# Output projection fed from a table, token sums in two pieces, and empty pulls in the final norm

## The chip, the cores and the metric

The kernel runs on one core of a Trainium2 chip. The metric is the device time of one execution in microseconds (us). The profile is of one such execution; its span runs from the program's first instruction to its last. TensorE (PE) does the matrix products, VectorE (DVE) and ScalarE (ACT) the elementwise work, GpSimd (POOL) some of it, and SyncE's queue (SP) issues all DMA transfers.

## The reference

One layer over 128 context tokens and 2048 latent tokens, 2176 in all, with a model width of 1024. Context and latent tokens get their own modulation vectors (`v` 0 or 1 in the kernel).

```python
h = rmsnorm(x, norm1) * (1 + scale1) + shift1
z = h @ w_in                       # short-convolution inputs, q, k, v, o, gates
y_sc = sc_b * conv3(sc_c * sc_x)   # along a row of 64 tokens
h_m = mlstm_bidir(q, k, v, gates)  # 4 heads, 16 chunks of 128 tokens, both directions
h_m = normed(h_m) * sigmoid(o)
x = x + gate1 * (concat([y_sc, h_m]) @ w_out)
h2 = rmsnorm(x, norm2) * (1 + scale2) + shift2
up = conv3(h2 @ w_up)              # down the columns of the grid
x = x + gate2 * ((silu(gg) * a) @ w_down)
y = rmsnorm(x, final_norm)
```

The final states of the context scan are returned too.

## The kernel before

Activations lie with features on the 128 partitions and tokens along the free dimension. Every float32 product is made of three: each operand is split into a rounded part (`H`, `wh`, by a copy on ACT) and a rest (`L`, `wl`, by a subtraction on VectorE or GpSimd), and high by high, high by low and low by high are summed in PSUM. `gemm` (L221 to L223) does this for 8 feature tiles and a block of up to 384 tokens, 24 products in all. There are six token blocks; the last has 256 tokens. Weights come through `load_w`: a DMA into `wst`, the copy `wh` on ACT (L127) and two half subtractions `wl` on GpSimd (L130).

The order of the front half. After the modulation and the first norm, blocks 3 to 5 and then 0 to 2 get their values, gates, keys, queries, output gates and short convolution. The last such stretch weaves two sequences. `weave` walks over units, calls the named stages of several units in the order of its list, and pulls items from a generator `fill` at a given rate. First the units are `Sums` (backward states) with the fill `heads` for queries and output gates; then they are `Mix` (one chunk and head pair each) at 1.6 items a unit, with the fill `shortconv` (36 items: four feature tiles by three blocks by three products) followed by `out_proj` (48 steps).

`out_proj` runs over three groups of two token blocks; a step is one `gemm` of one output tile for one block, and its eviction (L604) adds the residual row on VectorE. Its input, the mixed features in DRAM (`yD`), is loaded in two halves of four tiles, and split into `yH` and `yL` by `split_y`: four copies (L517) and four subtractions (L518) in a row. For blocks 0 and 1 `shortconv` calls this through `load_y`, for the others `out_proj` pulls `next_y`, four tiles at a time. `close` stores a finished row and squares it (L566), `add` sums the squares (L572), and `stats` makes the second norm's factors from them (L493 to L495).

From the first unit of `Mix` to the end of `out_proj`, `in_order` ties each engine, and SP's queue, to the order in which the code emits the instructions. Outside this stretch a planner orders each engine's instructions by priority and a cost model, with the emission order as the priority.

The up projection works with sums and differences of token and weight quarters, seven products in place of eight, in two halves of the tokens. `sums` forms the seven token forms for half of such a half (`qs`), in four rounds `kk`: load two stretches of `xD` into a tile `F`, norm and modulate them (L272, L274), form the differences (L276 to L279), split the ones named in `direct` into their slots (L283, L284) and store the rest to `tD` (L287). `split` loads a form from `tD` into `F` (L302) and splits it into its slot (L312, L313). The slots are used in the order 6, 0, 1, 5, 2, 4, 3. `F` has two buffers.

The down projection is built in the same way, in two groups `g` of seven products `i`, each over eight pairs `k` of output tile and token part. `close` adds the result to the residual and sums squares. `finish` makes the final norm of half a part: `inv_rms` (products L144, VectorE L147, a power on GpSimd L148), `spread` (products L155), and eight multiplications (L1331) with a store each. These generators are chained in `after`, and pulled four items at a time behind the products of each `k` from 2 on:

```python
if k >= 2:
    for _ in islice(after, 4):
        pass
```

## Time and profile before

| what | value |
|---|---|
| time, median of 3 runs | 2541.38 us (2538.63 to 2546.69) |
| profiled execution | 2547.02 us, its span 2545.2 us |
| mean granted TensorE clock | 0.987 |
| TensorE products busy | 2464.8 us, 97% of the span |
| VectorE, ACT, GpSimd busy | 1664.6, 1122.8, 573.7 us |

The profile names an engine's instruction by its line in the code and by the tiles it writes and reads. A wait is the idle time of an engine in front of an instruction and is put down to what released it. The granted clock is the share of full speed at which TensorE was allowed to run.

### The profile page before, as it was taken

How to read it: one execution, taken by the hardware profiler on the slowest of the kernel's cores; microseconds unless marked ns; L12 is line 12 of the kernel's file. 1: busy time of each engine (PE TensorE's matmuls, PEld its weight loads, DVE VectorE, ACT ScalarE, POOL GpSimd, SP SyncE). 2: the span in 40 equal slices, each digit the busy share in tenths (PEclk: the TensorE clock that was granted, in tenths of full speed). 3: DMA queues.
4: the chain of work that ended last, by engine and by line, in shares of the span. 5: the costliest groups of instructions: out<-in, count | busy, mean ns of one | idle time of the engine just before them, and what ended most of it. 6: DMA issues, size and time to landing. Idle time of an engine off the chain costs nothing.

```text
span 2545.2 us, 42525 instructions
## 1 busy us (share of the span) xinstructions
PE 2464.8 (97%) x16127; PEld 2360.4 (93%) x16127; DVE 1664.6 (65%) x2670; ACT 1122.8 (44%) x2059; POOL 573.7 (23%) x501
## 2 busy tenths in 40 slices
PE   7999999998999999889999999899999999999998
PEld 7999999998999989889999999788888899999998
DVE  3993552331556676688677666877767786787586
ACT  4421162333444554455444444555545554444342
POOL 2442242110343443322122111221221100000000
PEclk9999999999999999999999999999999999999999
DMA  8873873455666876755224122522222276867674
GB/s 282 279 241 116 305 242 96 126 177 166 209 208 204 285 243 221 250 199 174 83 99 165 73 74 83 183 98 84 92 98 84 80 248 207 251 195 225 188 222 133
DMA packets 281424, 444.60 MB, mean 175 GB/s; under 512 B 23283, under 2 KB 206723, under 8 KB 279555
## 3 DMA queue, kind: packets, MB, share of 16 engines
q1 hardware_dynamic: 281218, 441.88, 52.9%
q8 instruction: 127, 2.08, 0.3%
q14 instruction: 79, 0.64, 0.1%
HBM read 335.31 MB, written 106.48 MB: 174 GB/s over the span
## 4 chain that ended last, share of the span: by engine, by line
PE 68%; DVE 5%; DMA 4%; issue 2%; ACT 1%; POOL 0%; SPq 0%; DVEq 0%; ACTq 0%; POOLq 0%
PE pa L1206 7%; PE pa L1208 6%; PE pa L1207 6%; PE d L1361 5%; PE d L1362 5%; PE d L1360 5%; PE acc L221 4%; PE acc L223 4%; PE acc L222 4%; PE pb L1206 3%; PE pb L1207 3%; PE pb L1208 3%; PE pc L1206 2%; PE pc L1207 2%; PE pc L1208 2%
## 5 line engine op out<-in xcount | busy, mean ns | idle before, releaser
L221 PE MATMUL acc<-hH,wh 128*128 128x384 f32 (+1 forms) x1536 | 514.6, 335 | 23.3 <-DVE row L604 14.6
L223 PE MATMUL acc<-hH,wl 128*128 128x384 f32 (+1 forms) x1536 | 507.8, 331 | 0.4 <-POOL wl L130 0.4
L222 PE MATMUL acc<-hL,wh 128*128 128x384 f32 (+1 forms) x1536 | 506.7, 330 | 0.0
L1206 PE MATMUL pa<-tH,wh 128*128 128x288 f32 (+1 forms) x1056 | 348.7, 330 | 12.1 <-issue 7.3
L1360 PE MATMUL d<-bh,wh 128*128 128x272 f32 x1232 | 356.7, 290 | 0.7 <-ACT raw L1218 0.7
L1362 PE MATMUL d<-bh,wl 128*128 128x272 f32 x1232 | 357.1, 290 | 0.0
L1361 PE MATMUL d<-bl,wh 128*128 128x272 f32 x1232 | 356.3, 289 | 0.0
L1208 PE MATMUL pa<-tH,wl 128*128 128x288 f32 (+1 forms) x1056 | 347.9, 329 | 1.0 <-DVE wl L331 1.0
L1207 PE MATMUL pa<-tL,wh 128*128 128x288 f32 (+1 forms) x1056 | 347.6, 329 | 0.0
L331 POOL TENSOR_TENSOR wl<-st,wh 128x512 fp32r<-128x512 f32 x132 | 185.3, 1403 | 704.3 <-ACT wh L330 677.8
L130 POOL TENSOR_TENSOR wl<-wst,wh 128x512 fp32r<-128x512 f32 (+1 forms) x160 | 236.5, 1501 | 419.2 <-ACT wh L127 373.1
L221 PEld LDWEIGHTS acc<-hH,wh 128*128 128x128 f32 x1536 | 292.6, 190 | 26.2 <-issue 15.4
L222 PEld LDWEIGHTS acc<-hL,wh 128*128 128x128 f32 x1536 | 292.8, 191 | 0.3 <-issue 0.2
L223 PEld LDWEIGHTS acc<-hH,wl 128*128 128x128 f32 x1536 | 292.0, 190 | 1.1 <-POOL wl L130 0.9
L1149 DVE SCALAR_TENSOR_TENSOR tt<-raw,fw,tt 128x127 f32<-128x127 f32 (+4 forms) x264 | 246.4, 955 | 2.7 <-ACT tt L1155 1.4
L1360 PEld LDWEIGHTS d<-bh,wh 128*128 128x128 f32 x1232 | 232.9, 189 | 1.3 <-ACT raw L1218 1.1
L1361 PEld LDWEIGHTS d<-bl,wh 128*128 128x128 f32 x1232 | 232.9, 189 | 0.2
L1362 PEld LDWEIGHTS d<-bh,wl 128*128 128x128 f32 x1232 | 232.9, 189 | 0.0
L1206 PEld LDWEIGHTS pa<-tH,wh 128*128 128x128 f32 x1056 | 199.3, 189 | 28.8 <-issue 8.3
L1208 PEld LDWEIGHTS pa<-tH,wl 128*128 128x128 f32 x1056 | 199.9, 189 | 17.0 <-DVE wl L331 1.4
L1207 PEld LDWEIGHTS pa<-tL,wh 128*128 128x128 f32 x1056 | 199.5, 189 | 15.6
L330 ACT ACTIVATE wh<-s 128x512 fp32r<-128x512 f32 x176 | 110.9, 630 | 175.2 <-PE pc L1207 92.6
(248 smaller groups left out, 4849.8 us busy)
## 6 DMA issues: line engine op xcount, KB each, us to landing
st<-in_w_up SPq DMA_DIRECT2D x88, 512.0 KB, 3.9
us<-uD SPq DMA_DIRECT2D x48, 544.0 KB, 4.9
wst<-in_w_in SPq DMA_DIRECT2D x48, 512.0 KB, 4.9
uD<-tt SPq DMA_DIRECT2D x44, 544.0 KB, 2.7
R<-nD SPq DMA_DIRECT2D x34, 512.0 KB, 4.2
wm<-in_w_modr SPq DMA_DIRECT2D x32, 512.0 KB, 5.5
wst<-in_w_out SPq DMA_DIRECT2D x24, 512.0 KB, 6.9
st<-wsD SPq DMA_DIRECT2D x32, 384.0 KB, 3.5
```

The costliest lines, as they stand in the source:

```text
L130: G.tensor_sub(wl[:, a:a + n // 2], st[:, a:a + n // 2], wh[:, a:a + n // 2].bitcast(F32))
L221: PE.matmul(acc[:, :n], w_h, hH[:, k, :n], start=(k == 0), stop=False)
L222: PE.matmul(acc[:, :n], w_h, hL[:, k, :n], start=False, stop=False)
L223: PE.matmul(acc[:, :n], w_l, hH[:, k, :n], start=False, stop=(k == KT - 1))
L331: (G if on_pool else V).tensor_sub(wl, a, wh.bitcast(F32))
L1149: V.scalar_tensor_tensor(o, i, w, o, op0=ALU.mult, op1=ALU.add)
L1206: PE.matmul(acc, wh[:, w], rh, start=(kk == 0 and i in (0, 1, 5)), stop=False, skip_group_check=True)
L1207: PE.matmul(acc, wh[:, w], rl, start=False, stop=False, skip_group_check=True)
L1208: PE.matmul(acc, wl[:, w], rh, start=False, stop=(kk == 3), skip_group_check=True)
L1360: PE.matmul(acc, wh[:, c], uh, start=(kk == 0), stop=False)
L1361: PE.matmul(acc, wh[:, c], ul, start=False, stop=False)
L1362: PE.matmul(acc, wl[:, c], uh, start=False, stop=(kk == KH - 1))
```

## The change

The change has these parts:

- The first three weights of the second short convolution are loaded by `ahead_w`, behind 10 of the 12 items of the output gates, and no longer when the convolution starts.
- `Feed` replaces `load_y`, `split_y` and `next_y`. It holds a table from step to loads (`load`), copies (`lead`, four at a time) and subtractions (`trail`, two or three at a time). `shortconv` and `out_proj` call it at the start and at the end (`late`) of each step; steps 0 to 35 are the convolution, 36 to 83 the projection.
- The update of the forward state in `Mix.denom` becomes a stage `state` of its own, behind `heads`.
- `sums` loads two `F` tiles ahead, multiplies both stretches by the row factors in one instruction, lets ACT apply scale and bias together, and yields between this and the differences. A pass has nine yields in place of eight.
- Slot 0 is made before the first pass, so both passes fill slots 6 and 0 directly, and the first half of slot 0 is no longer stored and loaded again. The passes are pulled by `until`, one yield a step. `stats` of a group comes a step earlier.
- The value rows of `vg` use the pool of `row` with six buffers in place of four of their own.
- `finish` yields three times between `inv_rms` and `spread`, and ACT copies the spread factors to SBUF for the multiplications. In the last `k` of the kernel nine items are pulled in place of four.

```diff
@@ -259,19 +259,20 @@
...
-            nf = load(0)
+            fs = [load(0), load(1)]
             yield
             for kk in range(4):
-                f = nf
-                if kk < 3:
-                    nf = load(kk + 1)
-                for i, k in ((4, kk + 4), (6, kk)):
-                    x = f[:, i * w:(i + 2) * w]
-                    for i0, n, v in ((0, P, 0), (P, 2 * w - P, 1)) if ts[0] == 0 else ((0, 2 * w, 1),):
-                        e = i0 + n
-                        V.scalar_tensor_tensor(x[:, i0:e], x[:, i0:e], ab[:, 1, k, v:v + 1], rb[:, i0:e],
-                                               op0=ALU.mult, op1=ALU.mult)
-                        S.activation(x[:, i0:e], x[:, i0:e], AF.Identity, bias=modT[:, 24 + k, v:v + 1])
+                f = fs.pop(0)
+                x = f[:, 4 * w:8 * w].rearrange("p (a t) -> p a t", a=2)
+                V.tensor_tensor(x, x, bc(rb[:, None, :2 * w], [P, 2, 2 * w]), op=ALU.mult)
+                for i, k in enumerate((kk + 4, kk)):
+                    for a, e, v in spans(ts[0], ts[0] + 2 * w):
+                        a, e = a - ts[0], e - ts[0]
+                        S.activation(x[:, i, a:e], x[:, i, a:e], AF.Identity, bias=modT[:, 24 + k, v:v + 1],
+                                     scale=ab[:, 1, k, v:v + 1])
+                if kk in (1, 2):
+                    fs.append(load(kk + 1))
+                yield
                 f = f[:, :8 * w].rearrange("p (i t) -> p i t", t=w)
@@ -282,11 +283,9 @@
...
                     V.tensor_sub(tl[:, c0:c1], f[:, i], th[:, c0:c1].bitcast(F32))
-                yield
                 i0, i1 = int(0 in direct), 7 - int(6 in direct)
                 Q.dma_start(tDs[hf][i0:i1, :, c0:c1].rearrange("i p t -> p i t"), f[:, i0:i1])
-                if kk < 3:
-                    yield
+                yield
@@ -387,7 +386,7 @@
...
                             PE.matmul(acc[:, :264], a_l, w_h, start=False, stop=(k == KT - 1))
-                        r = rq.tile([P, 2, 129], F32, name="rv", bufs=4)
+                        r = rp.tile([P, 384], F32, name="row")[:, :258].rearrange("p (h d) -> p h d", h=2)
                         G.memset(r[:, :, 128:129], 1.0)
@@ -418,12 +417,16 @@
...
-        def shortconv(blocks, hs, then=None, more=(), ws=None):
+        def first_w(blocks):
+            return [load_w(I["w_in"][o]) for o in (4, 8, 0)]
...
+        def shortconv(blocks, hs, more=(), ws=None, hook=None):
             todo = chain((I["w_in"][o + m] for m in range(4) for o in (4, 8, 0)), more)
-            ws = [] if ws is None else ws
-            ws += [load_w(next(todo)) for _ in range(3)]
+            ws = first_w(blocks) if ws is None else ws
+            todo = islice(todo, 3, None)
+            hook = hook or (lambda late=False: None)
             got, stores = [], []
@@ -445,8 +448,7 @@
...
                     store()
-                    if then and m == 3 and j:
-                        then(j - 1, 0)
+                    hook()
                     acc = gemm(wc, hs[b], n)
...
@@ -469,9 +473,9 @@
...
                         split()
-                    if then and m == 3 and j:
-                        then(j - 1, 1)
+                    hook(True)
                     yield
+                    hook()
                     acc = gemm(wb, hs[b], n)
...
@@ -496,53 +499,47 @@
         done, early = set(), {}
-        def get_y(b):
...
-        def split_y(b, yts, kh):
...
-        def load_y(b, step):
-            if step == 0:
-                held_y[b] = get_y(b)
-                if b:
-                    next(outs)
-            else:
-                split_y(b, held_y[b], step - 1)
-        def next_y(grp, ready):
...
+        class Feed:
+            def __init__(self, grps):
+                self.step, self.plan, self.yt = 0, {}, {}
+                for g, (a, b) in enumerate(grps):
+                    for b_, at in ((a, ((-8, 0, self.load, 1), (-6, 0, self.load, 0), (-6, 1, self.lead, 1),
+                                        (-5, 0, self.trail, (4, 5)), (-4, 0, self.trail, (6, 7)), (-4, 1, self.lead, 0),
+                                        (-3, 0, self.trail, (0, 1)), (-2, 0, self.trail, (2, 3)))),
+                                   (b, ((-3, 0, self.load, 1), (-2, 1, self.load, 0), (-2, 1, self.lead, 1),
+                                        (-1, 0, self.trail, (4, 5, 6)), (-1, 1, self.lead, 0),
+                                        (0, 0, self.trail, (7, 0, 1)), (1, 0, self.trail, (2, 3))))):
+                        for k, late, f, arg in at:
+                            self.plan.setdefault((36 + 16 * g + k, late), []).append((f, b_, arg))
+            def __call__(self, late=False):
+                for f, b, arg in self.plan.get((self.step, int(late)), ()):
+                    f(b, arg)
+                self.step += late
+            def load(self, b, kh):
+                assert done >= set(chunks(b))
+                t0, n = BL[b]
+                yt = self.yt[b, kh] = xp.tile([P, 4, 384], F32, name="xt")
                 Q.dma_start(yt[:, :, :n], yD[4 * kh:4 * kh + 4, :, t0:t0 + n].rearrange("k p t -> p k t"))
+            def lead(self, b, kh):
+                n = BL[b][1]
+                if kh:
+                    early[b] = h_pair()
+                for k in range(4):
+                    S.activation(early[b][0][:, 4 * kh + k, :n], self.yt[b, kh][:, k, :n], AF.Copy)
+            def trail(self, b, ks):
+                n = BL[b][1]
+                yH, yL = early[b]
+                for k in ks:
+                    V.tensor_sub(yL[:, k, :n], self.yt[b, k // 4][:, k % 4, :n], yH[:, k, :n].bitcast(F32))
+        def out_proj(grps, defer, ws, hook):
@@ -571,15 +568,13 @@
...
-            rows, got, behind, squared, held, sss, past = [], [], [], [], [], {}, set()
+            rows, got, behind, squared, held, sss = [], [], [], [], [], {}
             for k in range(2):
                 load_r(k)
-            ny = iter(())
             yield
...
                 grp, (t0, n) = grps[g], BL[b]
-                if k % 16 == 0 and g + 1 < len(grps):
-                    ny = next_y(grps[g + 1], (lambda: True, lambda b=grp[0]: (b, KT - 1) in past))
+                hook()
                 load_r(k + 2)
@@ -591,27 +586,24 @@
...
                 w, xr = ws[m % 2], rows.pop(0)
-                if k % 16 >= 5:
-                    next(ny, None)
                 acc = gemm(w, early[b], n)
...
                     del ws[:2]
-                if held and k == held[0] + 5:
+                if held and k == held[0] + 4:
                     stats(held[1], [sss[b] for b in held[1]])
...
                                            op0=ALU.mult, op1=ALU.add)
-                past.add((b, m))
                 behind.append((b, m, xr))
                 if k % 16 == 15:
-                    run(ny)
                     held = [k, grp]
...
                     defer.append(lambda: stats(grp, [sss[b] for b in grp]))
+                hook(True)
                 yield
@@ -988,12 +980,7 @@
...
             def denom(self):
-                c, hp, sf = self.c, self.hp, sfs[self.hp]
-                if 0 <= c < NL - 1:
-                    for h in range(2):
-                        r = c * 4 + 2 * hp + h
-                        V.scalar_tensor_tensor(sf[:, h], sf[:, h], decB[:, r:r + 1], self.sb[:, h, 0],
-                                               op0=ALU.mult, op1=ALU.add)
+                c, hp = self.c, self.hp
                 yv = self.yv = self.y[:, :, :258].rearrange("p h (d n) -> p h d n", d=2)
@@ -1012,6 +999,14 @@
...
+            def state(self):
+                c, hp, sf = self.c, self.hp, sfs[self.hp]
+                if 0 <= c < NL - 1:
+                    for h in range(2):
+                        r = c * 4 + 2 * hp + h
+                        V.scalar_tensor_tensor(sf[:, h], sf[:, h], decB[:, r:r + 1], self.sb[:, h, 0],
+                                               op0=ALU.mult, op1=ALU.add)
@@ -1079,38 +1074,49 @@
...
         wo = []
-        outs = out_proj(((0, 1), (2, 3), (4, 5)), late, wo)
-        fill = chain(heads(BA, hs, 12, qD, AF.Copy, QS), heads(BA, hs, 20, oD, AF.Sigmoid, 1.0))
+        grps = ((0, 1), (2, 3), (4, 5))
+        feed = Feed(grps)
+        outs = out_proj(grps, late, wo, feed)
+        feed.plan.setdefault((33, 0), []).append((lambda *_: next(outs), None, None))
+        og = heads(BA, hs, 20, oD, AF.Sigmoid, 1.0)
...
+        def ahead_w():
+            wo.extend(first_w(BA))
+            return
+            yield
...
+        fill = chain(heads(BA, hs, 12, qD, AF.Copy, QS), islice(og, 10), ahead_w(), og)
         with tc.tile_pool(name="ms", bufs=1, side="right") as ms:
...
         run(fill)
-        fill = chain(shortconv(BA, hs, load_y, [I["w_out"][m] for m in range(2)], wo), islice(outs, 37))
+        fill = chain(shortconv(BA, hs, [I["w_out"][m] for m in range(2)], wo, feed), outs)
         mb = phr.enter_context(tc.tile_pool(name="mb", bufs=1, side="right"))
...
                (-1, "out"), (0, "scores"), (-3, "turn"), (0, "queries"), (-2, "norm"), (-1, "denom"), (0, "weigh"),
-               (-3, "third"), (-1, "heads"), (-2, "scale"), (1, "exps")))
+               (-3, "third"), (-1, "heads"), (-1, "state"), (-2, "scale"), (1, "exps")))
         phr.close()
...
+        def until(k, side):
...
+            while feed.step < 36 + k:
+                next(fill)
+                next(side, None)
+            run(side)
...
         fpool = phf.enter_context(tc.tile_pool(name="fpool", bufs=1, side="right"))
-        slots = {6: slot(6, "right")}
-        side = sums(0, fpool, (0,), (6,))
-        for _ in fill:
-            next(side, None)
+        slots = {i: slot(i, "right") for i in (6, 0)}
+        until(36, sums(0, fpool, (0,), (6, 0)))
+        run(islice(fill, 1))
         ph0.close()
-        slots[0] = slot(0, "right")
         fp = ph2.enter_context(tc.tile_pool(name="fp", bufs=1, side="right"))
         st = get_up(0)
-        for _ in chain(side, sums(0, fpool, (1,), (6, 0))):
-            run(islice(outs, 1))
-        f = get_f(0, 0, (0,))
-        run(islice(outs, 1))
-        put_f(f, 0, 0, (0,))
-        run(islice(outs, 1))
+        until(46, sums(0, fpool, (1,), (6, 0)))
         prods = stages(st)
         ahead = [next(prods) for _ in range(2)]
-        run(outs)
+        run(fill)
         in_order(first)
@@ -1325,10 +1331,14 @@
...
             inv_rms(ss, NB, r)
-            rb = spread(r, NB)
+            for _ in range(3):
+                yield
+            ps = spread(r, NB)
+            rb = dp.tile([P, NB], F32, name="rb", bufs=2)
+            S.activation(rb, ps[:, :NB], AF.Copy)
             for m in range(KT):
                 q = outs[m, p][:, half * NB:(half + 1) * NB]
-                V.scalar_tensor_tensor(q, q, nrm[:, 2, m:m + 1], rb[:, :NB], op0=ALU.mult, op1=ALU.mult)
+                V.scalar_tensor_tensor(q, q, nrm[:, 2, m:m + 1], rb, op0=ALU.mult, op1=ALU.mult)
                 Q.dma_start(O["y"][m][:, t0:t0 + NB], q)
@@ -1392,7 +1402,7 @@
...
                     if k >= 2:
-                        for _ in islice(after, 4):
+                        for _ in islice(after, 4 if g == 0 or i < 6 or k < 7 else 9):
                             pass
```

More of the change, by code (lines that the diff above doesn't have):

```diff
@@ L481, in shortconv @@
                         get()
-                    if then and m == 3 and j:
-                        then(j - 1, 2)
+                    hook(True)
                     yield
@@ L497, in hymba_kernel @@
         done, early = set(), {}
-        def get_y(b):
-            assert done >= set(chunks(b))
-            t0, n = BL[b]
-            yts = []
-            for kh in range(2):
-                yt = xp.tile([P, 4, 384], F32, name="xt")
-                Q.dma_start(yt[:, :, :n], yD[4 * kh:4 * kh + 4, :, t0:t0 + n].rearrange("k p t -> p k t"))
-                yts.append(yt)
-            return yts
-        def split_y(b, yts, kh):
-            n = BL[b][1]
-            if kh == 0:
-                early[b] = h_pair()
-            yH, yL = early[b]
-            for k in range(4):
-                S.activation(yH[:, 4 * kh + k, :n], yts[kh][:, k, :n], AF.Copy)
-                V.tensor_sub(yL[:, 4 * kh + k, :n], yts[kh][:, k, :n], yH[:, 4 * kh + k, :n].bitcast(F32))
@@ L520, in hymba_kernel @@
-        held_y = {}
-        def load_y(b, step):
-            if step == 0:
-                held_y[b] = get_y(b)
-                if b:
-                    next(outs)
-            else:
-                split_y(b, held_y[b], step - 1)
-        def next_y(grp, ready):
-            for b, may in zip(grp, ready):
-                while not done >= set(chunks(b)):
-                    yield
-                yts = get_y(b)
-                yield
-                for kh in range(2):
-                    while not may():
-                        yield
-                    split_y(b, yts, kh)
-                    yield
@@ L544, in out_proj @@
-        def out_proj(grps, defer, ws):
+        class Feed:
[18 more added lines that the diff above has]
+                yt = self.yt[b, kh] = xp.tile([P, 4, 384], F32, name="xt")
+                Q.dma_start(yt[:, :, :n], yD[4 * kh:4 * kh + 4, :, t0:t0 + n].rearrange("k p t -> p k t"))
+            def lead(self, b, kh):
[9 more added lines that the diff above has]
+                    V.tensor_sub(yL[:, k, :n], self.yt[b, k // 4][:, k % 4, :n], yH[:, k, :n].bitcast(F32))
@@ L580, in out_proj @@
                 grp, (t0, n) = grps[g], BL[b]
-                if k % 16 == 0 and g + 1 < len(grps):
-                    ny = next_y(grps[g + 1], (lambda: True, lambda b=grp[0]: (b, KT - 1) in past))
+                hook()
                 load_r(k + 2)
@@ L614, in out_proj @@
                     defer.append(lambda: stats(grp, [sss[b] for b in grp]))
+                hook(True)
                 yield
```

## The prediction

> **What bounds the kernel now.** I read the span first, then who waited for whom on TensorE, then single gaps in order of time, then the granted clock around them.
>
> ```profile
> span 2545.2 us, 42525 instructions
> PE 2464.8 (97%) x16127; PEld 2360.4 (93%) x16127; DVE 1664.6 (65%) x2670; ACT 1122.8 (44%) x2059; POOL 573.7 (23%) x501
> ```
>
> TensorE's products fill 97% of the span, and the change removes none of them. What it can win is TensorE's idle time, 2545.2 - 2464.8 = 80 us, plus what a lowered clock takes after a gap. The waits, as total, times and longest:
>
> ```profile
> PE acc L221 <- DVE row L604: 14.6, 6, 3.9
> PE acc L221 <- ACT wh L127: 8.2, 1, 8.2
> ...
> PE pa L1206 <- issue: 7.3, 1, 7.3
> PE st L155 <- POOL fr L148: 4.5, 4, 2.0
> PE y L988 <- DVE R L976: 3.5, 3, 1.3
> ...
> PE y L986 <- DVE R L972: 2.8, 1, 2.8
> ```
>
> All six belong to code that the diff touches; together they are 40.9 us. Granted clock (third last column) in stretches behind such gaps:
>
> ```profile
> 629.75:636.45 6.70, 6.30 (x18) 5.79 (x19) 0.00 (x0) 1.79 (x2) 4.99 (x4) 0.50 0.32 95
> 900.00:910.00 10.00, 10.00 (x60) 10.00 (x60) 7.85 (x25) 5.62 (x21) 0.94 (x2) 0.87 1.05 371
> 950.00:960.00 10.00, 10.00 (x58) 10.00 (x57) 7.45 (x22) 5.47 (x21) 0.94 (x2) 0.83 0.64 191
> 1106.40:1111.70 5.30, 5.29 (x25) 5.30 (x26) 5.27 (x8) 4.10 (x7) 0.00 (x0) 0.57 0.81 294
> 2265.00:2270.00 5.00, 4.71 (x21) 4.38 (x20) 2.65 (x7) 0.84 (x1) 0.92 (x1) 0.50 0.90 295
> 2270.00:2275.00 5.00, 5.00 (x37) 5.00 (x36) 3.22 (x8) 1.17 (x2) 0.00 (x0) 0.86 0.35 117
> ```
>
> Length times (1 - clock) is what TensorE lost there: 3.35, 1.3, 1.7, 2.3, 2.5 and 0.7 us. A gap costs itself and this.
>
> **A, the short convolution's first three weights.** Before, they are loaded when its first product is due; after, two products earlier (`ahead_w`, behind 10 of 12 output-gate items).
>
> ```profile
> 611.44 0.32 SPq L405 DMA_DIRECT2D oD<-row  x1
> ...
> 622.72 0.32 SPq L405 DMA_DIRECT2D oD<-row  x1
> 623.14 12.03 SPq L119 DMA_DIRECT2D wst<-in_w_in  x4
> ```
> ```profile
> 628.64 1.06 ACT L127 ACTIVATE wh<-wst 128x1024 fp32r<-128x1024 f32 x1 [1.51 <-DMA wst<-in_w_in]
> ```
>
> Today the loads stand on SP's queue behind the last row's store (622.72) and the first is split from 628.64. In the new order they stand behind the store two rows earlier, at 611.44: 11.3 us, against a wait of 8.2. The split waits on ACT behind the DMA, and the next row's eviction is behind it; a second accumulator covers that. GpSimd's three splits of the weights move with them, into a stretch where that engine, 23% busy overall, has little else. Gain 8.2 + 3.35 = 11.6 at most; I take 11, bounds 6 (ACT's wait passes on half) and 11.6.
>
> **B, the state update behind the heads.** In `Mix.denom` it stood ahead of the denominators and, on VectorE's queue, of `weigh` (L976).
>
> ```profile
> 676.97 2.68 DVE L995 SCALAR_TENSOR_TENSOR sf<-sf,decB,sb 128x129 f32<-128x129 f32 x2
> ```
>
> The same two instructions now come after `heads`. They still run before the next unit's `queries` (L972). At stake are 3.5 + 2.8 us of waits; the 2.8 has the input loads of part C as its other half. I take 4, between 0 (the update only delays L972 instead) and 6.3.
>
> **C, the projection's inputs by table.** The same 48 copies and 48 subtractions run; four copies and four subtractions came together, after it four copies at a step's end and two or three subtractions at the start of the next.
>
> ```profile
> 892.60 4.92 DVE L518 TENSOR_TENSOR hL<-xt,hH 128x384 fp32r<-128x384 f32 x4 [3.71 <-ACT hH L517]
> ```
> ```profile
> 892.23 2.87 POOL L130 TENSOR_TENSOR wl<-wst,wh 128x512 fp32r<-128x512 f32 x2 [6.81 <-ACT wh L127]
> ```
> ```profile
> 898.20 0.42 PE L221 MATMUL acc<-hH,wh 128*128 128x384 f32 x1 [2.66 <-DVE row L604]
> 949.49 0.42 PE L221 MATMUL acc<-hH,wh 128*128 128x384 f32 x1 [3.68 <-DVE row L604]
> ```
>
> The four took 4.92 us with GpSimd at work on L130, and the eviction L604 stood behind them. Two at that pace are 2.5 us. How long is a step? The 24 products of one:
>
> ```profile
> 600.49 0.42 PE L221 MATMUL acc<-hH,wh 128*128 128x384 f32 x1
> ...
> 604.59 0.34 PE L223 MATMUL acc<-hH,wl 128*128 128x384 f32 x1
> ```
>
> First start to last is 4.1 us, 4.2 with the last. So 2.5 us fits beside an eviction. Both gaps with their clock are 2.66 + 3.68 + 1.3 + 1.7 = 9.3; I take 7, down to 2 if copies, now emitted at a step's end, hold ACT's work for the next unit of `Mix`.
>
> [...]
>
> **D, token sums in two pieces, each with a step between.** One `tensor_tensor` of 128x1152 replaces two (or four) scalings; ACT takes scale and bias in one instruction; the first pass also fills slot 0 directly. Waits here are the rest of L604's 14.6, 8.3 us. VectorE's prices:
>
> ```profile
> 987.20 1.96 DVE L518 TENSOR_TENSOR hL<-xt,hH 128x384 fp32r<-128x384 f32 x4
> 989.07 0.61 DVE L604 SCALAR_TENSOR_TENSOR row<-acc,modT,row 128x384 f32<-128x384 f32 x1
> 989.60 0.55 DVE L572 TENSOR_TENSOR cr<-cr,sq 128x384 f32<-128x384 f32 x1
> ...
> 1061.46 0.46 DVE L276 TENSOR_TENSOR F<-F 128x288 f32<-128x288 f32 x1 [0.84 <-ACT F L274]
> 1061.95 0.95 DVE L277 TENSOR_TENSOR F<-F 128x288 f32<-128x288 f32 x1
> 1062.94 0.46 DVE L279 TENSOR_TENSOR F<-F 128x288 f32<-128x288 f32 x1
> 1063.31 0.82 DVE L284 TENSOR_TENSOR tL<-F,tH 128x288 fp32r<-128x288 f32 x2
> ...
> 1107.63 1.35 DVE L313 TENSOR_TENSOR tL<-F,tH 128x1152 fp32r<-128x1152 f32 x1
> ```
>
> The new pass takes nine steps, and both input blocks of the last group fall into seven of them. Estimate from these rows: 9 x (0.61 + 0.55) = 10.4; subtractions 8 x 0.49 and, for the narrower block, 8 x two thirds of it, 6.5; sums 4 x (1.35 + 0.46 + 0.95 + 0.46 + 0.82) = 16.2. That is 33.1 us in nine steps of 4.2, 37.8. Part C showed GpSimd stretching VectorE 2.5 times, so some 6 us more is likely: VectorE is just full. The second pass has no subtractions of inputs. So the first pass keeps about its stalls and the second loses them: 5, from -2 (VectorE stretched by 12 us in the first pass, 45 against 37.8, and 3 left in the second) to 8.3.
>
> **E, into the up projection.** Before, half of slot 0 went to DRAM and back, and its split stood ahead of the last evictions:
>
> ```profile
> 1091.41 4.27 DMA tD<-F
> ...
> 1095.76 5.80 DMA F<-tD
> ```
> ```profile
> F<-tD SPq DMA_DIRECT2D x5, 1152.0 KB, 5.7
> ```
>
> The 7.3 us gap, with its clock 9.6, ends as the last L604 frees the accumulators. That round trip goes. But slots 1, 5, 2, 4, 3 still make it: store to landing 4.27, load 5.8, two splits of 1.35. Two F buffers allow two loads at a time: slot 1 is ready 4.3 + 5.8 + 1.2 + 1.35 = 12.6 us behind the last store (1.2 is ACT's copy, estimated a little under the subtraction). Slot 3 comes two rounds of a buffer later, 2 x (5.8 + 1.2 + 2.7) = 19.4, at 32.
>
> ```profile
> 1200.00:1250.00 50.00, 50.00 (x377) 50.00 (x377) 34.34 (x55) 24.48 (x43) 7.78 (x6) 1.00 0.20 70
> ```
>
> In this settled stretch of the up projection a product takes 50 / 377 = 0.133 us. TensorE would want slot 3, the seventh, after two last steps of 2.8 (the narrow block, two thirds of 4.2) and six times 24 products, 3.2 each: 25. So some 7 of the 9.6 us are only passed on to the slots, and the store comes a step later than now. I take 2, from -3 to 9.6.
>
> **F, the final norm.** The three empty pulls separate the sums from the spread only where a round of four pulls ends between them. For the first finish of either group the fourth pull of the same round makes the spread, so nothing comes between:
>
> ```profile
> 2264.52 1.16 PE L155 MATMUL st<-ident,fr 128*128 128x128 f32 x4 [2.01 <-POOL fr L148]
> ...
> 2306.53 1.03 PE L155 MATMUL st<-ident,fr 128*128 128x128 f32 x6 [1.12 <-POOL fr L148]
> ```
>
> The 2.01 stays, the 1.12 goes. The end pays: the last but one finish, now behind the last product, puts eight more multiplications near the tail, which closes so:
>
> ```profile
> 2540.03 1.72 DVE L1331 SCALAR_TENSOR_TENSOR bot<-bot,nrm,st 128x272 f32<-128x272 f32 x4
> ```
>
> At most 8 x 0.43 = 3.4, less what hides in the pow and spread. I take 0 for F, -3.4 to 5.6 (1.12, 2.01 and 2.5 of clock). The `rv` rows from the larger pool cost nothing by themselves: stage one's stores hide under products; uncovered, one wait of about one of their stores.
>
> **The sum.** 11 + 4 + 7 + 5 + 2 + 0 = 29 us. The profiled execution took 2547.0 for a span of 2545.2, so 2518 for its like; it lay 5.6 above the median. From the median 2541.4: 2512.4.
>
> **The rivals.** First, the stall moves: VectorE stays full through the sums and the slots starve. Then A holds (11), B and C give 3 together, D takes 2 and E takes 3: 9 us, 2532. For it speaks the 33 of 38 us under D; against it, that VectorE is busy only 65% overall. Second, everything named goes: 11.6 + 6.3 + 9.3 + 8.3 + 9.6 + 1.1 = 46, 2495. Against it stands the slot chain of E. Third, slower: the final stage's order is planned, not written, and with later emission and an added copy on ACT the spread is placed ahead of a late pow in all finishes, as it is in the first one today. The price each is that of 2264.52: 2.0 and 2.5 + 0.7 of clock, 5.2. Seven more are 36.4: 2541.4 - 29 + 36.4 = 2549; it decides from six of them (29 / 5.2 = 5.6). Against it: the other seven cost 4.5 - 2.0 = 2.5 together now. Fourth, the separation in F does nothing at all: that is inside F's bounds.
>
> **Chances.** Forecast 0.60, first rival 0.20, second 0.10, third 0.10. A difference under 0.3%, 7.6 us, can't be told from none here. The first rival lies on that edge, so half of it counts as same; with a little of the forecast's tail: faster 0.78, same 0.13, slower 0.09. The range is 2498 to 2536, leaving out the slower case and half of the second rival.
>
> **What would show it.** A right: the wait on wh L127 near 622 is gone and the clock stays at 1.0. B: no wait of L988 on L976. C: pieces of two subtractions and no gap over 1 us up to 950. D: waits on L604 only in the first pass. E: small waits for tH and tL in the first block instead of one of 7.3. F: one wait near 2264, none near 2306, and an end chain with both last finishes. The forecast is wrong if TensorE's idle time between 600 and 1150 falls by less than 15 us, or if the final norm's waits exceed 10.

## The result, and the profile after

The changed kernel takes 2515.7 us (median of 4 runs, 2514.4 to 2516.3) against 2541.3: a ratio of 0.990, 95% interval 0.988 to 0.991. That is 25.6 us less; 2512.4 was forecast.

From the page of the changed kernel:

```profile
span 2513.7 us, 42486 instructions
```

The span fell by 31.5 us, more than the median, since the profiled execution of before lay 5.6 us above its median; so up to some 6 of the 31.5 can belong to that execution and not to the change. Where the 31.5 went shows in three groups of products: those of `Mix` on the values (`y<-v,R`), of the up and of the down projection. Each row has the count, the durations, then first and last start. First of the kernel before, then of the changed one:

```profile
L988 PE MATMUL y<-v,R x272: 272/275/583, 646.4 to 967.9; 128*128 128x129 f32 x136
L1206 PE MATMUL pa<-tH,wh x1056: 288/297/628, 1106.4 to 2046.7; 128*128 128x288 f32 x118, 128*128 128x512 f32 x58
L1360 PE MATMUL d<-bh,wh x1232: 282/288/428, 2048.3 to 2532.3; 128*128 128x272 f32 x176
```
```profile
L980 PE MATMUL y<-v,R x272: 272/275/276, 636.4 to 940.4; 128*128 128x129 f32 x136
L1212 PE MATMUL pa<-tH,wh x1056: 288/297/628, 1070.0 to 2015.7; 128*128 128x288 f32 x118, 128*128 128x512 f32 x58
L1370 PE MATMUL d<-bh,wh x1232: 282/288/428, 2017.2 to 2496.5; 128*128 128x272 f32 x176
```

| stretch | before, us | after, us | difference |
|---|---|---|---|
| start to the first product of `Mix` | 646.4 | 636.4 | -10.0 |
| `Mix`, first to last of these products | 321.5 | 304.0 | -17.5 |
| from there to the first product of the up projection | 138.5 | 129.6 | -8.9 |
| from there to the first of the down projection | 941.9 | 947.2 | +5.3 |
| down projection, to its last product | 484.0 | 479.3 | -4.7 |
| last product to the end | 12.9 | 17.2 | +4.3 |

So 36.4 us were won ahead of the up projection, more than the whole change shows; 5.3 us were given back inside it, and the final norm only moved time from inside to the end. The gain up to the end of `Mix` is seen in TensorE's share of one stretch (stretch, length, then busy time of PE; the granted clock is the third last column). Before, then after:

```profile
600.00:950.00 350.00, 328.77 (x2084) 325.64 (x2083) 195.34 (x436) 163.60 (x488) 138.20 (x140) 0.98 0.70 224
```
```profile
600.00:950.00 350.00, 350.00 (x2269) 348.97 (x2269) 189.53 (x470) 177.07 (x529) 147.11 (x149) 1.00 0.72 233
```

TensorE has no idle time left from 600 to 950 us, where it had 21.2. The main gaps that remain behind it, from the timeline of the changed kernel (start, duration, instruction, idle time before it and its releaser):

```profile
982.52 0.41 PE L221 MATMUL acc<-hH,wh 128*128 128x384 f32 x1 [1.37 <-DVE row L597]
1004.20 0.66 PE L221 MATMUL acc<-hH,wh 128*128 128x384 f32 x1 [2.74 <-DVE row L597]
1070.00 0.58 PE L1212 MATMUL pa<-tH,wh 128*128 128x288 f32 x1 [3.80 <-ACT sq L563]
1089.08 0.40 PE L1212 MATMUL pa<-tH,wh 128*128 128x288 f32 x1 [0.66 <-ACT tH L311]
1111.07 0.40 PE L1214 MATMUL pb<-tH,wl 128*128 128x288 f32 x1 [1.08 <-DVE wl L330]
1114.81 0.40 PE L1212 MATMUL pa<-tH,wh 128*128 128x288 f32 x1 [0.81 <-ACT wh L329]
1118.67 0.40 PE L1214 MATMUL pc<-tH,wl 128*128 128x288 f32 x1 [2.54 <-POOL wl L330]
```

The eviction of the output projection (L597, L604 before) is still waited for, in the first pass of the sums alone; four short waits for weights (0.36 to 1.25 us) have come in between; the 7.29 us ahead of the up projection are 3.80; and in its second block stand three waits for weights that the kernel before does not have. The tail, with both last finishes in it, of the changed kernel:

```profile
2498.88 1.03 PE L155 MATMUL st<-ident,fr 128*128 128x128 f32 x6 [1.32 <-POOL fr L148]
...
2500.38 1.74 DVE L1341 SCALAR_TENSOR_TENSOR top<-top,nrm,rb 128x272 f32<-128x272 f32 x4 [1.10 <-ACT rb L1338]
...
2502.03 1.73 DVE L1341 SCALAR_TENSOR_TENSOR bot<-bot,nrm,rb 128x272 f32<-128x272 f32 x4
...
2503.68 0.21 DVE L147 TENSOR_SCALAR fr<-st 128x2 f32<-128x2 f32 x2
2503.91 1.21 POOL L148 TENSOR_TENSOR fr<-fr,mhalf 128x2 f32<-128x2 f32 x2 [4.57 <-DVE fr L147]
2504.66 1.76 PE L155 MATMUL st<-ident,fr 128*128 128x128 f32 x6 [3.53 <-POOL fr L148]
```

The sums of the very last finish wait in the accumulator for VectorE's L147, which stands behind eight multiplications of the finish before it (2500.38 to 2503.76). From the last product to the last spread it takes 8.2 us (2496.5 to 2504.66) where the kernel before took 4.8 (2532.3 to 2537.10): that is 3.4 of the 4.3 us. The other 0.9 lie behind it: the spread takes 1.76 us where it took 1.25, and ACT's copy of 0.40 us stands between it and the multiplications.

### The profile page after: what moved, and what is told of

The parts are those of the page before. It is cut to its first block, busy times and chain, and to the rows that moved or that the text cites. A ratio compares the mean times of both kernels' runs of the same rounds, so it can differ in the third digit from the quotient of the medians.

```text
span 2513.7 us, 42486 instructions
## 1 busy us (share of the span) xinstructions
PE 2456.8 (98%) x16127; PEld 2353.7 (94%) x16127; DVE 1634.1 (65%) x2649; ACT 1125.9 (45%) x2070; POOL 579.0 (23%) x501
## 4 chain that ended last, share of the span: by engine, by line
PE 85%; DVE 6%; DMA 4%; issue 2%; ACT 2%; POOL 1%; SPq 0%; DVEq 0%; POOLq 0%; ACTq 0%
PE acc L221 9%; PE acc L223 9%; PE acc L222 9%; PE pa L1212 6%; PE pa L1214 6%; PE pa L1213 6%; PE d L1370 6%; PE d L1372 6%; PE d L1371 5%; PE pb L1212 3%; PE pb L1214 3%; PE pb L1213 3%; PE pc L1212 2%; PE pc L1214 2%; PE pc L1213 2%
## 5 line engine op out<-in xcount | busy, mean ns | idle before, releaser
L1370 PE MATMUL d<-bh,wh 128*128 128x272 f32 x1232 | 356.9, 290 | 0.7 <-ACT raw L1224 0.7
L1370 PEld LDWEIGHTS d<-bh,wh 128*128 128x128 f32 x1232 | 232.6, 189 | 1.4 <-ACT raw L1224 1.1
```

Of the source, the lines that this page charges most:

```text
L1370: PE.matmul(acc, wh[:, c], uh, start=(kk == 0), stop=False)
```

## The experiments

The theory is the prediction's sum: each part removes waits of its own, so undoing one brings back its term. Its main rival is that the stall only moves, so that undoing a part costs little. The marks are starts of the first product of the up and of the down projection in each run's trace, and its span. Two lengths are taken from the same traces: `Mix`, from the first to the last of its products `y<-v,R`, and "to up", from there to the first product of the up projection.

| run | edit | median, us | ratio to before [95%] | `Mix` | to up | first up | first down | span |
|---|---|---|---|---|---|---|---|---|
| kernel before | | 2541.3 | | 321.5 | 138.5 | 1106.4 | 2048.3 | 2545.2 |
| changed kernel | | 2515.7 | 0.990 [0.988, 0.991] | 304.0 | 129.6 | 1070.0 | 2017.2 | 2513.7 |
| e1 | A undone | 2522.4 | 0.993 [0.991, 0.994] | 304.0 | 129.4 | 1079.6 | 2025.3 | 2519.0 |
| e2 | B undone | 2513.9 | 0.990 [0.988, 0.991] | 305.5 | 129.4 | 1070.2 | 2015.9 | 2510.4 |
| e3 | C's pieces undone | 2523.6 | 0.993 [0.992, 0.995] | 311.7 | 131.1 | 1081.2 | 2026.4 | 2520.9 |
| e4 | D's two pieces undone | 2520.3 | 0.992 [0.990, 0.993] | 304.0 | 137.4 | 1079.0 | 2022.6 | 2520.3 |
| e5 | F undone | 2513.9 | 0.990 [0.989, 0.992] | 304.0 | 129.5 | 1069.3 | 2015.5 | 2514.1 |
| e6 | F drawn out | 2513.3 | 0.989 [0.987, 0.991] | 304.0 | 129.5 | 1072.2 | 2017.0 | 2508.8 |
| e7 | evictions ahead of weights | 2510.2 | 0.989 [0.987, 0.990] | 304.0 | 127.5 | 1067.2 | 2013.6 | 2507.9 |
| e8 | second half's sums later | 2509.1 | 0.988 [0.986, 0.989] | 304.0 | 129.5 | 1071.9 | 2011.4 | 2509.4 |
| e9 | kernel before, with B alone | 2530.6 | 0.995 [0.994, 0.997] | 310.6 | 134.1 | 1093.3 | 2032.9 | 2529.8 |
| e10 | e7 and e8 | 2506.4 | 0.987 [0.985, 0.988] | 304.0 | 127.5 | 1070.2 | 2010.6 | 2504.8 |
| e11 | e6, e7 and e8 | 2502.7 | 0.985 [0.984, 0.987] | 304.0 | 127.4 | 1068.6 | 2007.6 | 2500.6 |
| e12 | B and C's pieces undone | 2526.2 | 0.995 [0.994, 0.997] | 317.8 | 131.5 | 1086.2 | 2031.2 | 2525.3 |

An interval is some 4 us wide to either side, so times closer than that are not told apart by the medians; the marks are one trace each. They differ by 2 to 3 us between kernels that are alike up to there (e7 and e10: 1067.2 and 1070.2). That scatter lies ahead of `Mix`, whose first product comes at 635.7 in e7 and at 638.7 in e10. The `Mix` length hardly has it: it is 304.0 in all nine kernels that leave B and C as they are. So what a part does between there and the up projection is read from the two lengths.

**e1: A undone.**

```diff
-        fill = chain(heads(... 12 ...), islice(og, 10), ahead_w(), og)
+        fill = chain(heads(... 12 ...), og)
...
-            ws = first_w(blocks) if ws is None else ws
+            ws = first_w(blocks) if ws is None else ws.extend(first_w(blocks)) or ws
```

> The changed kernel with one part undone: the first three weights of the short convolution are loaded at its own start again, behind the heads' last rows. Theory (each wait removed was a loss of its own): the wait for wh L127 near 620 us comes back with 8 us and a granted clock below 1 behind it, first up-projection product 9 to 12 us later, the kernel 9 to 12 us slower than the changed one (about 2526). Rival (later waits absorb it, since they stood on transfers that do not depend on this): less than 4 us slower.

From its timeline:

```profile
629.45 0.69 PE L221 MATMUL acc<-hH,wh 128*128 128x384 f32 x1 [7.80 <-ACT wh L127]
1079.65 0.37 PE L1212 MATMUL pa<-tH,wh 128*128 128x288 f32 x1 [3.91 <-ACT sq L563]
```

The wait is back, `Mix` starts 9.8 us later (646.2) and takes the same 304.0 us, and the 3.80 ahead of the up projection is 3.91, 9.6 us later. At the end 5 to 8 us are left of it (span 5.3, median 6.7, ratio 8), less than the theory's 9 to 12 and more than the rival's 4; the intervals don't tell that from 9.6. So the wait was a loss of its own as far as the up projection. Whether a part of it is absorbed later, the times don't show.

**e2, e3, e12: B and C's pieces, each undone and both.** In e2 and e12 the stage `state` is called right ahead of `denom`. In e3 and e12 each `lead` has its four subtractions right behind it:

```diff
-   (-6, 1, self.lead, 1), (-5, 0, self.trail, (4, 5)), (-4, 0, self.trail, (6, 7)), ...
+   (-6, 1, self.lead, 1), (-6, 1, self.trail, (4, 5, 6, 7)), ...
```

> The changed kernel with one part undone: VectorE's two state updates of a step stand ahead of the denominators again. Theory: waits of L988-type lines on VectorE come back between 600 and 900 us, some 3 to 6 us in all, and the kernel is 3 to 6 us slower than the changed one. Rival (the waits of before came from the missing first weights and from bursts of four subtractions, and the order inside the step did nothing): within 1 us of the changed kernel, no waits over 1 us before 950 us.

> The changed kernel with one part undone: the four subtractions of a half of the output projection's inputs stand in one step again, right behind their four copies. Theory: gaps of 2.5 to 4 us on TensorE near 898 and 949 us come back, with a granted clock of about 0.87 behind them; 5 to 9 us slower than the changed kernel. Rival (in the changed order of the steps VectorE has room for the four): 0 to 2 us slower, no gap over 1 us before 950 us.

> The changed kernel with two parts undone together: the state updates ahead of the denominators and pieces of four subtractions in one step. Undone alone, the first cost nothing and the second 8 us. Theory (the two parts make room on VectorE in the same steps, so either one covers part of the other's gaps): the two together cost clearly more than the sum, 12 to 18 us over the changed kernel (about 2528 to 2534), with gaps of 2.5 us or more on TensorE between 800 and 950 us. Rival (the parts are independent): 6 to 9 us, about 2523.

The gaps of 1 us or more up to 950 us that wait for VectorE, from the timelines of e2, e3 and e12 in this order:

```profile
669.66 0.49 PE L980 MATMUL y<-v,R 128*128 128x129 f32 x2 [1.28 <-DVE R L968]
```
```profile
827.46 0.49 PE L978 MATMUL y<-sf,R 128*128 128x129 f32 x2 [1.16 <-DVE R L964]
923.49 0.49 PE L978 MATMUL y<-sf,R 128*128 128x129 f32 x2 [1.16 <-DVE R L964]
```
```profile
671.27 0.49 PE L980 MATMUL y<-v,R 128*128 128x129 f32 x2 [1.29 <-DVE R L968]
828.28 0.49 PE L978 MATMUL y<-sf,R 128*128 128x129 f32 x2 [1.97 <-DVE R L964]
829.88 0.49 PE L980 MATMUL y<-v,R 128*128 128x129 f32 x2 [1.11 <-DVE R L968]
907.69 0.49 PE L980 MATMUL y<-v,R 128*128 128x129 f32 x2 [1.77 <-DVE R L968]
926.89 0.49 PE L978 MATMUL y<-sf,R 128*128 128x129 f32 x2 [1.66 <-DVE R L964]
```

In the `Mix` stretch B undone alone costs 1.5 us, C's pieces 7.7 and both 13.8, where 9.2 would be the sum: B is worth 6.1 us where the pieces are of four and 1.5 where they are of two or three. (At the first up product it is 0.2, 11.2 and 16.2, with the scatter ahead of `Mix` in it: of e3's 11.2, 2.0 lie ahead of `Mix` and 1.5 behind it.) By the ratios both cost 14 us, C's pieces alone 9. So theory e12 holds in kind, and at its lower end, but its gaps of 2.5 us or more don't come: the longest is 1.97. Theory e2 falls as written. In e3 the loss is as expected, but the gaps are smaller (1.16, not 2.5 to 4) and not at the eviction L597: VectorE is late for `Mix` (L964, L968) instead. Of its 7.7 us 4.3 are TensorE's idle time from 600 to 950 us; the rest was not followed further.

Why the two parts are not independent shows in VectorE's order ahead of e12's gaps at 828.28 and 829.88:

```profile
823.51 3.05 DVE L540 TENSOR_TENSOR hL<-xt,hH 128x384 fp32r<-128x384 f32 x4
826.48 1.74 DVE L964 TENSOR_TENSOR R<-R,q 128x512 f32<-128x512 f32 x1
828.15 0.60 DVE L1008 SCALAR_TENSOR_TENSOR sf<-sf,decB,sb 128x129 f32<-128x129 f32 x2
...
829.15 0.68 DVE L968 TENSOR_TENSOR R<-S,R 128x512 f32<-128x512 f32 x1
```

The four subtractions (C) stand ahead of L964, and the state updates (B) between L964 and L968. In e3, with the subtractions alone, TensorE waits 1.16 and 0.58 us at this step, against 1.97 and 1.11 here. (Of the 1.97 a part is L964 itself: it takes 1.74 us here, beside GpSimd's L947 from 826.17 for 1.51 us, and 0.68 in e3, where L947 has just ended.) In e2, with the updates alone (at 821.40), it waits for neither: there the subtractions come behind L968, at 823.85. So the updates cost TensorE time only where VectorE is late already. In the changed kernel updates and subtractions both follow L968 (821.27), at 822.71 and 823.90.

**e9: B alone, in the kernel before.** `Mix.denom` loses its two updates, which run as `state` behind `heads`.

> The kernel before with one part of the change alone: VectorE's two state updates stand behind the heads. Theory (undoing this part in the changed kernel cost nothing since the finer pieces of four had already made room on VectorE; in the kernel before the room was missing): two or more of the gaps of 1.05 to 3.68 us between 600 and 950 us get smaller by 1 us or more each, 2 to 5 us faster than before. Rival (the order inside the step never set TensorE's pace): within 1.5 us of the kernel before, the same gaps.

From its timeline:

```profile
838.40 0.49 PE L986 MATMUL y<-sf,R 128*128 128x129 f32 x2 [1.18 <-DVE R L972]
894.22 0.41 PE L221 MATMUL acc<-hH,wh 128*128 128x384 f32 x1 [2.25 <-DVE row L604]
942.41 0.41 PE L221 MATMUL acc<-hH,wh 128*128 128x384 f32 x1 [2.13 <-DVE row L604]
```

The gaps of before, 2.80, 2.66 and 3.68, are 1.18, 2.25 and 2.13; the two L988 waits ahead of 820 us are under 0.6. The kernel is 11 us faster than before by the medians (12 by the ratio, 0.995), and 10.9 us faster in `Mix`; 2 to 5 were expected, so the theory holds in kind and was too small. B moved TensorE's pace as long as VectorE had no room, at L604 too, which the prediction's B doesn't name. Another 4.4 us are won behind `Mix` (134.1 against 138.5), where no state update runs any more; what makes them was not followed.

**e4: D's two pieces undone.** The multiplication, ACT's scale, the differences, the direct splits and the store stand in one step, and the next holds nothing.

```diff
                     fs.append(load(kk + 1))
-                yield
...
                 Q.dma_start(tDs[hf][i0:i1, ...], f[:, i0:i1])
                 yield
+                yield
```

> The changed kernel with one part undone: one step's piece of the token sums holds the multiplication, the copies, the differences, the direct splits and the store, and the next step none. Theory: waits for the row eviction of the output projection (L597) in the second pass of the sums too, 3 to 8 us in all beyond the 4.1 us of the changed kernel, so 3 to 8 us slower. Rival (VectorE has the same work in two steps either way, and the two waits of the first pass have another cause): within 2 us of the changed kernel.

The groups of waits of e4 (releaser, total, times, longest), then its longest in the second pass:

```profile
PE acc L221 <- ACT sq L563: 10.2, 5, 3.1
...
PE acc L221 <- DVE row L597: 5.4, 2, 3.6
```
```profile
1046.51 0.42 PE L221 MATMUL acc<-hH,wh 128*128 128x384 f32 x1 [2.20 <-ACT sq L563]
1064.56 0.41 PE L221 MATMUL acc<-hH,wh 128*128 128x384 f32 x1 [2.17 <-ACT sq L563]
```

15.6 us of waits stand against 4.1 in the changed kernel (L597), in both passes; the 3.80 ahead of the up projection shrinks to 0.62. From the first spread of the sums to the first up product it takes 114.3 us, 106.6 with two pieces, 113.8 in the kernel before. Of the 9.0 us at the first up product 5.4 are left at the first down product, and 4.6 at the end by the medians. So the two steps make D's gain; how much of it is given back later lies within the intervals.

**e5, e6: the final norm as before, and drawn out.** In e5 the empty pulls and the nine pulls of the last product are taken out; ACT's copy of the spread factors stays. In e6 there are four empty pulls, and in the last seventh product the pulls start at once:

```diff
-            for _ in range(3):
+            for _ in range(4):
                 yield
...
-                    if i == 6 and k == 6:
+                    if i == 6 and k == 6 - g:
...
-                    if k >= 2:
-                        for _ in islice(after, 4 if g == 0 or i < 6 or k < 7 else 9):
+                    if k >= 2 or g and i == 6:
+                        for _ in islice(after, (4, 5, 7, 5, 3, 4, 8, 0)[k] if g and i == 6 else 4):
```

> The changed kernel with the final norm in the order of before: sums and spread in one piece, four pulls behind every product, the copy of the spread row kept. Theory: the wait of 1.1 us in the third finish (near 2275) and the one in the last product but one come back, but the two last finishes no longer run one behind the other at the end, so the end chain behind the last product falls from 16.6 to about 12.5 us: 0 to 3 us faster than the changed kernel. Rival (the separation is worth its waits): 1 to 4 us slower than the changed kernel.

> The changed kernel with the final norm drawn out further: four empty pulls, so that every sums block has a whole product behind it, and in the last seventh product the pulls start at once, so that the last finish but one is done before the last product ends. Theory (the separation works wherever a product really stands between, and the end pays only for the one finish that needs the last product): the wait of 1.6 us near 2233 goes, the tail behind the last product falls from 16.6 to about 12 us; 5 to 7 us faster than the changed kernel. Rival (VectorE's multiplications now collide with the evictions of the last products): waits for the evictions, less than 2 us gained.

The last spread of e5, then of e6:

```profile
2505.17 1.75 PE L155 MATMUL st<-ident,fr 128*128 128x128 f32 x6 [1.10 <-POOL fr L148]
```
```profile
2500.51 1.15 PE L155 MATMUL st<-ident,fr 128*128 128x128 f32 x6 [1.10 <-POOL fr L148]
```

The tail is counted from the start of the last product L1370 (L1368 in e5), as in the table above; the expectations count it from that stretch's end, 0.6 us less. In e5 the last product is 5.0 us longer in coming from the first down product (484.3 against 479.3) and the tail is 14.3 in place of 17.2, not the 12.5 expected; medians and intervals don't tell it from the changed kernel. In e6 the stretch stays at 479.1 and the tail is 12.7: 4.5 us are gained in the tail, with a span 4.9 shorter. The wait near 2233 is gone, but one of 1.95 us stands at 2286.58. The median shows 2.4, within the spread of its runs (2506 to 2517). The place is as the theory has it; its 5 to 7 us are not shown in the time.

**e7: the row evictions ahead of the weights.**

```diff
-        ahead = [next(prods) for _ in range(2)]
+        ahead = [next(prods)]
         run(fill)
+        ahead.append(next(prods))
```

> The changed kernel with one move: the second set of up-projection weights is made behind the last two steps of the output projection and not ahead of them, so that VectorE's last row evictions no longer stand behind it. Theory (the 3.8 us wait ahead of the first up-projection product is VectorE's order: the eviction that frees the accumulator stands behind the weights): the wait falls to about 2 us, the first up-projection product starts 2 us earlier and without the slow clock behind it; 2 to 4 us faster. Rival (the wait is handed on to the slots, which come from transfers): less than 1 us faster, the waits for tH near 1089 grow by what the first one loses.

From its timeline:

```profile
1067.21 0.37 PE L1213 MATMUL pa<-tH,wh 128*128 128x288 f32 x1 [1.89 <-ACT sq L563]
1085.27 0.40 PE L1213 MATMUL pa<-tH,wh 128*128 128x288 f32 x1 [0.65 <-ACT tH L311]
1088.56 0.40 PE L1214 MATMUL pa<-tL,wh 128*128 128x288 f32 x1 [0.64 <-DVE tL L312]
```

3.80 falls to 1.89, and from the end of `Mix` the up projection starts 2.1 us earlier (2.8 in absolute time). The slots take some of it back: waits on tH and tL of 0.65, 0.53 and 0.64 where there were 0.16 and 0.66. The theory holds for the wait, but not without the slow clock: it is 0.66 in the 5 us from 1067.20. 3.6 us are left at the first down product; the time, 3 us less by the ratios and 5.5 by the medians, is not clear of the intervals.

**e8: the second half's sums later.** The multiplications of the second half's pieces are tied behind what VectorE was given before them, out of the planner's hands.

```diff
-                V.tensor_tensor(x, x, bc(rb[:, None, :2 * w], [P, 2, 2 * w]), op=ALU.mult)
+                mul = V.tensor_tensor(x, x, bc(rb[:, None, :2 * w], [P, 2, 2 * w]), op=ALU.mult)
+                if hf:
+                    pin(mul)
```

> The changed kernel with one move: the multiplications of the second half's token sums are kept behind what VectorE was given before them, so that their first pieces leave the second block of the up projection. Theory (the three waits of 1.1, 0.8 and 2.5 us between 1111 and 1119 come from these pieces on VectorE and ScalarE): the waits go, 3 to 5 us faster than the changed kernel. Rival (they come from weights that land late): the waits stay, within 1 us.

The first multiplication of the second half, in the changed kernel and in e8:

```profile
1103.61 1.22 DVE L267 TENSOR_TENSOR F<-F,rb 128x1024 f32<-128x1024 f32 x1
```
```profile
1122.17 1.22 DVE L267 TENSOR_TENSOR F<-F,rb 128x1024 f32<-128x1024 f32 x1
```

The theory holds: the waits of 1.08, 0.81 and 2.54 are gone, and the up projection takes 939.5 us from first product to first down product in place of 947.2. That is where the 5.3 us given back had gone: the waits themselves are 4.4 of them. The other forms of the changed kernel that leave this order as it is take 943.6 to 947.2 us here, and e10 and e11, with the same move, 940.4 and 939.0. Why the kernel before has no such waits is not settled: its first pieces come 36 us behind its first up product, 34 in the changed kernel.

**e10, e11: e7 and e8 together, and with e6.**

> The changed kernel with two moves: the second set of up-projection weights behind the last two steps of the output projection, and the second half's token sums kept out of the second block of the up projection. Theory (two stalls at two places, independent): 5.5 us and 6.5 us add up to some 10 to 12 us, about 2505. Rival (the second stall was the first one's backlog, or the first one moves to the slots): 6 to 8 us, about 2509.

> The same two moves and the final norm drawn out over whole products, with the last finish but one done before the last product ends. Theory: 4 to 5 us below the kernel with the two moves alone (the tail of 16.6 us goes to 12.3, the waits of the first finish go), about 2500. Rival (what the final norm gains there lies within the spread of the runs and is taken back by a slower clock): 0 to 2 us.

e10 is 9.3 us below the changed kernel by the medians, between theory and rival, and 7 by the ratios, which is the rival's size. In the trace both gains are there: it is 2.1 us sooner at the up projection, counted from the end of `Mix`, as e7, and its up projection takes 940.4 us. e11 is the fastest of all, 37 us or 1.5% below the kernel before and 11 to 13 below the changed one. Its 3.8 us over e10 lie within the intervals, and the trace doesn't bear out the theory's 4 to 5: the tail is 13.0 where e10's is 17.1, but the stretch of the down projection is 480.0 where e10's is 477.1, which leaves 1.2 us, the rival's size.

## Why the prediction was right, step by step

- **The sum**: 29 forecast from the profiled execution, 31.5 measured there, 25.6 by the medians. It was right as a sum, partly by luck, since terms made up for each other: A 11 forecast and 10.0 measured, B and C 11 and 17.5, D and E 7 and 8.9, then 5.3 given back in the up projection, for which the sum has no term of its own, and F 0 and 0.4. TensorE's idle time from 600 to 1150 us fell from 39.6 to 17.5 us, by more than the 15 that the forecast asked for.
- **A**, 11 forecast: 10.0 up to the first product of `Mix`, 9.8 by e1. The sign held: no wait near 622, clock 1.00 from 600 to 950 us. The way there was another than forecast. The loads don't stand behind the store at 611.44: they are issued one by one, at 540.11, 557.55 and 575.64, the first of them here:

```profile
540.11 0.38 SPq L119 DMA_DIRECT2D wst<-in_w_in  x1
```

  So the place in the order of the items, which the prediction went by, is not what sets the time. Ahead of `Mix` the planner places the loads; in the kernel before they stood in the stretch whose order is tied, at 623.14, and A took them out of it.
- **B and C**, 4 and 7 forecast: 17.5 together in `Mix`. The step that failed is that each had gaps of its own, shared out by the line that waited. Both stand in VectorE's order in the same steps. B is worth 10.9 us in the kernel before (e9), 6.1 with C's pieces undone, and 1.5 in the changed kernel; and with B undone the rest of the change still wins 16.0 of the 17.5 (305.5 in e2 against 321.5). The sign of C, no gap over 1 us up to 950, held; and it held without B but for one gap of 1.28.
- **D**, 5 forecast, with **E**, 2: together 7.2, from the first spread of the sums to the first up product (113.8 to 106.6), and 8.9 from the end of `Mix`. The first pass keeps its stalls (3.86 before, 1.37 and 2.74 after) and the second loses them, as predicted from VectorE being just full. New there are waits for late weights, 0.36, 0.79, 1.25 and 0.73.
- **E**'s step was wrong. It passed 7 of 9.6 us on to the slots, by a chain of transfers that would have slot 3 ready at 32 us against 25 wanted. The slots cost 0.8 us. Half of the 3.80 us that stayed came from VectorE's order (e7), and the 5.3 given back from the second half's sums (e8). The slots showed their limit only once the start moved up by some 2 us (e7), and then by 1 us.
- **F**, 0 forecast: -4.7 in the stretch, +4.3 in the tail. The stretch is 476.5 to 480.9 us in the nine kernels with F as changed and 483.6 to 484.3 in the three without it, so its gain is real but spread over 3 to 8 us. The tail's price was bounded at 3.4 for eight multiplications; these cost 3.4, and the slower spread with ACT's copy, which the bound leaves out, 0.9.
- **The rivals**: the first, the stall moves, gave 9 us, and 25.6 came; e1, e3 and e4 each lost half or more of what their part had won. The second, everything named goes, gave 46 us; 31.5 came, and with three moves more (e11) the span is 44.6 below that of before. The third, a spread ahead of a late pow in all eight finishes, did not happen: TensorE waits for the pow in four places, 7.2 us in all, 4.8 of them behind the last product. The fourth, that F's separation does nothing, is open in the time: e5 is not told apart from the changed kernel.

## What to carry to other kernels

When several gaps wait for one nearly full engine, don't share them out by the line that waited: ask how much room each edit makes on that engine in that step, since the first edit that makes enough takes most of the gain of all (here 10.9 or 16.0 of 17.5). Behind a gap that closes, look at what the released engine does next; here the last evictions behind early weights, and pieces that a planner had drawn forward, cost 7 to 9 us that two small moves took back. An operation moved out of the stream of products is only hidden if something still runs behind it, so the one that goes last should be alone.

## What the runs showed of the hardware

The granted clock behind gaps of about the same length is not the same. In e4 a gap of 2.20 us ends at 1046.51 and one of 2.17 us at 1064.56. The 5 us behind each (busy time of PE behind the length, the granted clock third last):

```profile
1046.50:1051.50 5.00, 4.99 (x20) 5.00 (x21) 3.27 (x4) 2.07 (x3) 1.05 (x2) 0.66 1.02 354
1064.50:1069.50 5.00, 4.95 (x30) 4.98 (x31) 3.31 (x4) 2.07 (x3) 1.05 (x2) 1.00 0.50 168
```

TensorE has 20 products in the first and 30 in the second. The same for these and for other gaps, with the loss as in the prediction, length times (1 - clock):

| run | gap, us, and its end | stretch behind it | granted clock | loss there, us |
|---|---|---|---|---|
| e4 | 2.20, 1046.51 | 1046.50 to 1051.50 | 0.66 | 1.7 |
| e4 | 2.17, 1064.56 | 1064.50 to 1069.50 | 1.00 | 0 |
| e7 | 1.89, 1067.21 | 1067.20 to 1072.20 | 0.66 | 1.7 |
| e1 | 3.91, 1079.65 | 1079.60 to 1084.60 | 0.66 | 1.7 |
| changed kernel | 1.37, 982.52 | 982.50 to 987.50 | 1.00 | 0 |
| changed kernel | 2.74, 1004.20 | 1004.20 to 1009.20 | 0.71 | 1.5 |
| changed kernel | 3.80, 1070.00 | 1070.00 to 1075.00 | 0.50 | 2.5 |

So in these rows the length of a gap alone doesn't give the loss behind it: 2.20 us cost 1.7 more and 2.17 nothing, 1.89 and 3.91 the same 1.7. The 3.80 us cost 2.7 more, 2.5 as in the table and 0.2 from 1075 to 1080, where the clock is 0.96. What decides was not shown.
